# Moving the GEMM operands 32 bytes off the weights' place in SBUF, in a two-layer encoder trunk

## Chip, core and metric

The kernel runs on one core of one Trainium2 chip. The metric is the device time of one execution in microseconds (us), from launch to the last result. "Before" is the median of three timed runs; the trace is one further execution, recorded by the hardware profiler. Engines are named as in the profile: PE is the matrix engine, PEld its weight loads, DVE the vector engine, ACT the scalar engine, POOL the general-purpose one, SP the queue that issues the DMAs.

## The reference, cut to what matters

```python
D_MODEL, SEQ, DEPTH, D_FF = 2048, 256, 2, 8192
for i in range(DEPTH):
    u = rmsnorm(h, mix_norm_g[i])
    za, zh, zc, zr = split_last(u @ w_in[i], GROUP_SPLITS)      # 2048 x 6528
    ...                                                         # four mixers
    h = h + mix @ w_out[i]                                      # 2048 x 2048
    u = rmsnorm(h, mlp_norm_g[i])
    h = h + jnp.square(jax.nn.relu(u @ w_up[i])) @ w_down[i]    # 2048 x 8192, 8192 x 2048
    gate = jax.nn.sigmoid(rmsnorm(h, ple_norm_g[i]) @ w_ple_gate[i])   # 2048 x 2048
    h = h + (p[i] @ w_ple[i]) * gate
```

Everything is float32. There are 256 tokens, so each GEMM is a large weight matrix against a narrow activation.

## The kernel before

Activations lie transposed: channels on the 128 partitions, the 256 tokens (`S`) along the free axis, 16 chunks (`KC`) of 128 channels. Each GEMM keeps float32 accuracy with rounded operands (`F32R`): weight and activation are each split into a rounded part and the remainder. A weight unit of 1024 columns is loaded into `raw` (L135), ACT rounds each half of it into `wh` (L140) and DVE subtracts to get `wl` (L142). An activation chunk is a row of 512 columns, rounded part first and remainder behind it (`split`, L177).

One k-step multiplies one 128x128 weight block. There are two forms:

- `mm2` (L158, L159): `wh` against all 512 columns of the chunk, then `wl` against its first 256. Two weight loads and 768 columns.
- `mm3` (L150 to L152): three multiplications of 256 columns each (`wh` twice, `wl` once).

The weights are the stationary operand. The chunk of `u1`, `mh`, `u`, `act`, `ug` or `ph` is the moving operand, streamed past them. The next block's weights are loaded while a chunk streams.

The program runs stage after stage, twice, once for each layer:

- w_in and the mixers: moving operand `u1`, 15 output blocks by `mm3`, 36 by `mm2`, 16 k-steps each, between small float32 matmuls of the mixers.
- w_out: `mh1` by `mm2` (16 blocks of 12 k-steps), then `mh2` by `mm3` (16 blocks of 4).
- the MLP in four quarters: `up` (`u` into `act`) and `down` (`act` into `h`), each 16 blocks of 16 k-steps a quarter, all by `mm2`.
- the gate (`ug`, 16 blocks of 16 k-steps by `mm2`), mixed with w_ple (`ph`, 32 k-steps by `mm3`).

The moving operand `u` of a profile row is therefore one of two tiles (the profile drops numbers from names): `u1` in w_in, `u` in the MLP. Likewise `mh` is `mh1` at L158 and L159 and `mh2` at L150 to L152.

Tiles stand in pools, and a pool's place is set by the sizes of what was opened before it: `cp` (constants), `mp` (`h`, `u`, `ug`), `wp` (narrow weight buffers), then the pools of a stage (the wide weight buffers, `act`). The pool `up` with `u1` and `mh2`, and `op` with `mh1`, are allocated from the other end of SBUF. The order on each engine is the scheduler's; the functions below have the line numbers that the profile uses.

Of the kernel before, what the change touches and what calls it, by code (L numbers as in the profile page):

```python
# [8 lines left out]
F32 = mybir.dt.float32  # L9
# [7 lines left out]
P = 128  # L17
# [54 lines left out]
def trunk(ctx: ExitStack, tc: tile.TileContext, xT, pT, w_in, w_out1, w_out2, w_up, w_down, w_gate, w_ple, pvec,  # L72
          rel, lam, consts, lmask, onehot, lora, lorag, cw, outT, stages=None):
    nc = tc.nc
    V, A, G, T = nc.vector, nc.scalar, nc.gpsimd, nc.tensor

    cp = ctx.enter_context(tc.tile_pool(name="cp", bufs=1))
    mp = ctx.enter_context(tc.tile_pool(name="mp", bufs=1))
    wp = ctx.enter_context(tc.tile_pool(name="wp", bufs=3))
    sp = ctx.enter_context(tc.tile_pool(name="sp", bufs=4))  # L80
    pg = ctx.enter_context(tc.tile_pool(name="pg", bufs=2, space=PSUM))


    A.preload_act_table_set("natural_log_exp_and_others")
# [13 lines left out]
    def pc(l, n, i=0):  # L98
        o = l * NPC + POFF[n] + i
        return pv[:, o:o + 1]  # L100
# [60 lines left out]
    def add_to(dst, ps):  # L161
        V.tensor_tensor(dst, dst, ps[:, S:], ALU.add)
        V.tensor_tensor(dst, dst, ps[:, :S], ALU.add)  # L163

    def gemm_block(wsrc, m, act, mm=mm2, nk=KC, before=None):

        ps = K.accum("acc")
        for u in range(nk // 8):
            w = wsplit(wsrc[m, u])
            for j in range(8):  # L170
                k = u * 8 + j
                if before is not None:
                    before(k)
                mm(ps, w, j, act[:, k], k == 0, k == nk - 1)
        return ps

    def split(dst, src, scale=None):  # L177

        if scale is None:
            A.activation(dst[:, :S], src, AF.Copy)  # L180
            V.tensor_tensor(dst[:, S:], src, dst[:, :S].bitcast(F32), ALU.subtract)
        else:
            A.activation(dst[:, :S], src, AF.Identity, scale=scale)  # L183
            V.scalar_tensor_tensor(dst[:, S:], src, scale, dst[:, :S].bitcast(F32), ALU.mult, ALU.subtract)  # L184
# [36 lines left out]
    K = Ctx()  # L221
# [18 lines left out]
    def front():  # L240

        K.up_ = tc.tile_pool(name="up", bufs=1, side="right", reuse_waits="tile")
        K.up = K.up_.__enter__()
        K.u1 = K.up.tile([P, KC, 2 * S], F32R, tag="u1", name="u1")

    front()
    acc = sp.tile([P, S], F32, tag="ssacc", name="ssacc", bufs=1)

# [11 lines left out]
    for l in range(DEPTH):  # L260
# [53 lines left out]
        def norm():  # L314

            acc = sp.tile([P, S], F32, tag="ssacc", name="ssacc", bufs=1)
            for m in range(KC):
                sumsq(acc, h[:, m], m == 0)
            return rms_finish(acc, K.accum("ssq"))

        with tc.tile_pool(name="ap", bufs=2, reuse_waits="tile") as apool:
            NQ = 4
            acts, ahead, r = {}, [], None

            def up(q):
                nonlocal r
                acts[q] = apool.tile([P, 16, 2 * S], F32R, tag="act", name="act")
                if q == 0:
                    ahead.extend(gemm_block(w_up[l], f, u) for f in range(AHEAD))
                    r = norm()  # L330
                for f in range(16):
                    ps = ahead.pop(0) if ahead else gemm_block(w_up[l], q * 16 + f, u)
                    y = sp.tile([P, S], F32, tag="tmp", name="y", bufs=3)
                    A.activation(y, ps[:, S:], AF.Copy)
                    V.tensor_tensor(y, y, ps[:, :S], ALU.add)
                    V.scalar_tensor_tensor(y, y, 0.0, r, ALU.max, ALU.mult)
                    A.activation(y, y, AF.Square)
                    split(acts[q][:, f], y)

            def down(q):  # L340
                a = acts.pop(q)
                for m in range(KC):
                    ps = gemm_block(w_down[l, q], m, a)
                    add_to(h[:, m], ps)
                    if q == NQ - 1:
                        split(ug[:, m], h[:, m], pc(l, "pleg", m))
            up(0)
            for q in range(NQ):
                if q + 1 < NQ:
                    up(q + 1)  # L350
                else:
                    ug = mp.tile([P, KC, 2 * S], F32R, tag="u", name="ug")
                down(q)
# [12 lines left out]
        if l + 1 < DEPTH:  # L366
            front()
            acc = sp.tile([P, S], F32, tag="ssacc", name="ssacc", bufs=1)
# [75 lines left out]
class MixerD:  # L444
# [33 lines left out]
    def shift(self, m, blk, tag, bufs=1, ps=None):  # L478
        K, z, t = self.K, self.t1("z", 1), self.t1(tag, bufs)
        V, l, mu = K.nc.vector, K.l, K.pc  # L480
        if ps is None:
            K.z(m, z)
        else:
            V.tensor_tensor(z, ps[:, :S], K.r, ALU.mult)
        K.nc.scalar.activation(t, z, AF.Identity, scale=K.dcol(l, blk))
        V.scalar_tensor_tensor(t[:, 1:], z[:, :S - 1], mu(l, "mu0", blk), t[:, 1:], ALU.mult, ALU.add)
        V.scalar_tensor_tensor(t[:, :S - 1], z[:, 1:], mu(l, "mu1", blk), t[:, :S - 1], ALU.mult, ALU.add)
        return t
# [705 lines left out]
```

## Time and profile before

| | us |
|---|---|
| median of 3 runs | 2781.25 (2778.91 to 2785.14) |
| the profiled execution, its own time | 2778.84 |
| its span, first to last instruction | 2777.1 |
| PE busy | 2736.6 |
| DVE busy | 1986.5 |
| ACT busy | 1633.8 |

The recorded length of a matmul includes the drain of its results and overlaps the next one. The pace of PE is therefore read from the starts of neighbouring matmuls, not from their lengths; busy times of groups that alternate overlap and can't be added.

### The profile page before, as it was taken

How to read it: one execution, taken by the hardware profiler on the slowest of the kernel's cores; microseconds unless marked ns; L12 is line 12 of the kernel's file. 1: busy time of each engine (PE TensorE's matmuls, PEld its weight loads, DVE VectorE, ACT ScalarE, POOL GpSimd, SP SyncE). 2: the span in 40 equal slices, each digit the busy share in tenths (PEclk: the TensorE clock that was granted, in tenths of full speed). 3: DMA queues.
4: the chain of work that ended last, by engine and by line, in shares of the span. 5: the costliest groups of instructions: out<-in, count | busy, mean ns of one | idle time of the engine just before them, and what ended most of it. 6: DMA issues, size and time to landing. Idle time of an engine off the chain costs nothing.

```text
span 2777.1 us, 47281 instructions
## 1 busy us (share of the span) xinstructions
PE 2736.6 (99%) x16934; PEld 2361.7 (85%) x16934; DVE 1986.5 (72%) x4147; ACT 1633.8 (59%) x3342; POOL 54.5 (2%) x98
## 2 busy tenths in 40 slices
PE   8999999999999999999999999999999999999999
PEld 7878888888888888888898778888888888888887
DVE  8779777776666666677877797777766666666776
ACT  6656566566645546456765765565665465564565
POOL 0000110000000000000000011100000000000000
PEclk9999999999999999999999999999999999999999
DMA  6544454665555555555555454456655555555555
GB/s 221 169 132 159 152 166 151 218 199 184 189 183 189 185 187 187 185 189 192 175 168 162 140 165 142 164 163 191 195 185 188 185 189 184 189 186 186 186 198 160
DMA packets 187363, 495.45 MB, mean 178 GB/s; under 512 B 43860, under 2 KB 67028, under 8 KB 187000
## 3 DMA queue, kind: packets, MB, share of 16 engines
q1 hardware_dynamic: 187128, 492.44, 54.6%
q8 instruction: 133, 2.18, 0.3%
q14 instruction: 102, 0.84, 0.1%
HBM read 472.56 MB, written 19.80 MB: 177 GB/s over the span
## 4 chain that ended last, share of the span: by engine, by line
PE 89%; DVE 5%; ACT 2%; DMA 2%; issue 1%; SPq 0%; DVEq 0%; ACTq 0%
PE acc L158 49%; PE acc L159 25%; PE acc L152 2%; PE acc L150 2%; PE acc L151 2%; DVE wl L142 2%; PE psam L592 1%; PE psbl L1026 1%; ACT wh L140 1%; PE pss L757 1%; PE psrv L604 0%; DMA ot<-o_scr 0%; PE psy L780 0%; PE psl L936 0%; PE psrv L608 0%
## 5 line engine op out<-in xcount | busy, mean ns | idle before, releaser
L140 ACT ACTIVATE wh<-raw 128x512 fp32r<-128x512 f32 x1704 | 1076.5, 633 | 978.9 <-PE acc L158 831.1
L142 DVE TENSOR_TENSOR wl<-raw,wh 128x512 fp32r<-128x512 f32 x1704 | 1177.1, 692 | 631.4 <-ACT wh L140 620.4
L158 PE MATMUL acc<-u,wh 128*128 128x512 f32 x3200 | 1152.1, 401 | 4.9 <-ACT wh L140 4.0
L159 PE MATMUL acc<-u,wl 128*128 128x256 f32 x3200 | 917.9, 287 | 5.9 <-DVE wl L142 4.9
L158 PEld LDWEIGHTS acc<-u,wh 128*128 128x128 f32 x3200 | 601.2, 188 | 144.6 <-ACT wh L140 7.0
L158 PE MATMUL acc<-act,wh 128*128 128x512 f32 x2048 | 723.9, 399 | 0.0
L159 PEld LDWEIGHTS acc<-u,wl 128*128 128x128 f32 x3200 | 604.0, 189 | 23.9 <-DVE wl L142 16.4
L159 PE MATMUL acc<-act,wl 128*128 128x256 f32 x2048 | 575.2, 281 | 0.0
L158 PEld LDWEIGHTS acc<-act,wh 128*128 128x128 f32 x2048 | 384.8, 188 | 96.1
L159 PEld LDWEIGHTS acc<-act,wl 128*128 128x128 f32 x2048 | 386.9, 189 | 0.0
L158 PE MATMUL acc<-ug,wh 128*128 128x512 f32 x512 | 181.7, 398 | 0.0
L150 PE MATMUL acc<-u,wh 128*128 128x256 f32 x480 | 138.0, 287 | 10.7 <-ACT u L183 8.3
L152 PE MATMUL acc<-u,wl 128*128 128x256 f32 x480 | 140.8, 294 | 3.5 <-DVE wl L142 3.2
L159 PE MATMUL acc<-ug,wl 128*128 128x256 f32 x512 | 143.5, 281 | 0.0
L151 PE MATMUL acc<-u,wh 128*128 128x256 f32 x480 | 137.0, 285 | 0.8 <-DVE u L184 0.6
L158 PE MATMUL acc<-mh,wh 128*128 128x512 f32 x384 | 137.0, 396 | 0.7 <-DVE h L163 0.7
L158 PEld LDWEIGHTS acc<-ug,wh 128*128 128x128 f32 x512 | 96.0, 188 | 21.1
L159 PE MATMUL acc<-mh,wl 128*128 128x256 f32 x384 | 109.9, 287 | 1.4 <-DVE wl L142 1.2
L150 PEld LDWEIGHTS acc<-u,wh 128*128 128x128 f32 x480 | 91.3, 190 | 13.3 <-ACT u L183 8.3
L152 PEld LDWEIGHTS acc<-u,wl 128*128 128x128 f32 x480 | 91.0, 190 | 11.5 <-DVE wl L142 8.9
L159 PEld LDWEIGHTS acc<-ug,wl 128*128 128x128 f32 x512 | 96.7, 189 | 0.7
L151 PEld LDWEIGHTS acc<-u,wh 128*128 128x128 f32 x480 | 91.2, 190 | 2.0 <-DVE u L184 1.7
(321 smaller groups left out, 2738.4 us busy)
## 6 DMA issues: line engine op xcount, KB each, us to landing
raw<-in_w_up SPq DMA_DIRECT2D x256, 512.0 KB
raw<-in_w_down SPq DMA_DIRECT2D x256, 512.0 KB
raw<-in_w_in SPq DMA_DIRECT2D x204, 512.0 KB
raw<-in_w_gate SPq DMA_DIRECT2D x64, 512.0 KB
raw<-in_w_out SPq DMA_DIRECT2D x32, 512.0 KB
raw<-in_w_out SPq DMA_DIRECT2D x64, 256.0 KB
h<-in_xT SPq DMA_DIRECT2D x8, 512.0 KB
m_scr<-sp SPq DMA_DIRECT2D x16, 256.0 KB
```

Of the source, the lines that this page charges most:

```text
L140: A.activation(wh[:, :n], raw[:, o:o + n], AF.Copy)
L142: V.tensor_tensor(wl[:, :n], raw[:, o:o + n], wh[:, :n].bitcast(F32), ALU.subtract)
L150: T.matmul(ps[:, :S], w1, act[:, :S], start=start, stop=False)
L151: T.matmul(ps[:, :S], w1, act[:, S:], start=False, stop=False)
L152: T.matmul(ps[:, :S], w2, act[:, :S], start=False, stop=stop)
L158: T.matmul(ps, wh[:, b * P:(b + 1) * P], act, start=start, stop=False)
L159: T.matmul(ps[:, :S], wl[:, b * P:(b + 1) * P], act[:, :S], start=False, stop=stop)
L592: T.matmul(pm[h][:, x * S:(x + 1) * S], BK[HS[h], j, x, :], KR[j][HS[h]].rearrange("p a b -> p (a b)"), start=True, stop=True)
L757: T.matmul(ps[:, d * P + h * 64:d * P + (h + 1) * 64], Zs[d][:, h * 2 + j, :], rk(d, j)[:, h] if st == 0 else RH[:, d, h, :], start=True, ...
L1026: T.matmul(p2[:, i * P:(i + 1) * P], kc[:, i * P:(i + 1) * P], strided(Q, i * P, [[2 * hh, P // (2 * hh)], [W + hh, 2], [1, hh]]), start=T ...
```

## The change

It adds empty tiles ahead of four pools' contents. `shift` allocates one tile of the given number of float32 columns and sets it to zero once, so that the scheduler sees it used.

```diff
+    def shift(pool, cols):
+
+        V.memset(pool.tile([P, cols], F32, tag="pad", name="pad", bufs=1), 0.0)
+
+    shift(cp, 24)
+    shift(wp, 24)
...
         K.u1 = K.up.tile([P, KC, 2 * S], F32R, tag="u1", name="u1")
+        shift(K.up, 16)
...
         with tc.tile_pool(name="ap", bufs=2, reuse_waits="tile") as apool:
+            shift(apool, 8)
```

`shift(K.up, ...)` and `shift(apool, ...)` run once in each layer, so six memsets are added in all. No matmul, DMA or conversion is added, removed or changed in order; what changes is the byte address of nearly every tile in its partition. For the operands of the GEMMs the built programs place:

```
tile (where it moves or is weight)   before        mod 128   after         mod 128
wh, wl narrow (w_in, first of w_out)  96448...          64    96640...           0
wh, wl wide (w_out on, MLP, gate)    127168...          64   127360...           0
u1, mh2 (w_in, w_out by mm3)         196576             96   196512             32
mh1 (w_out by mm2)                   172000             96   171936             32
u, ug (up, gate)                      47296             64    47392             32
act, two buffers (down)              143552, 176320     64   143776, 176544     32
ph (w_ple)                           145600             64   145792              0
```

A chunk is 2048 bytes and a weight block 512, so all chunks of a tile and all blocks of a buffer have the same place modulo 128. The moving operand's place less the weights' is 32 bytes before for `u1`, `mh1` and `mh2`, and 0 for `u`, `ug`, `act` and `ph`. After the change it is 32 for all but `ph`, where it stays 0.

The order differs on DVE alone. This is the last part of w_out in layer 0, where `act`'s pool opens, before (`h`, `u`, `ssacc` and `sq` belong to the residual and its sum of squares):

```order
L184 SCALAR_TENSOR_TENSOR u<-h,pv,u 128x256
L308 TENSOR_TENSOR h<-h,acc 128x256
L142 TENSOR_TENSOR wl<-raw,wh 128x512
L184 SCALAR_TENSOR_TENSOR u<-h,pv,u 128x256
L142 TENSOR_TENSOR wl<-raw,wh 128x512
```

And the same place after the change, where all lines of the file stand 7 or 8 further down:

```order
L191 SCALAR_TENSOR_TENSOR u<-h,pv,u 128x256
L316 TENSOR_TENSOR h<-h,acc 128x256
L85 MEMSET pad 128x8
L149 TENSOR_TENSOR wl<-raw,wh 128x512
L191 SCALAR_TENSOR_TENSOR u<-h,pv,u 128x256
L149 TENSOR_TENSOR wl<-raw,wh 128x512
```

One memset has come in between two instructions whose order is as it was; its other places, two at the start, one behind the first constants and one in the gate of layer 0, look the same.

## Rows read from the trace of the kernel before

**Rows 1.** The page: span, PE's busy time, the chain that ended last by engine.

```profile
span 2777.1 us, 47281 instructions
PE 2736.6 (99%) x16934; PEld 2361.7 (85%) x16934; DVE 1986.5 (72%) x4147; ACT 1633.8 (59%) x3342; POOL 54.5 (2%) x98
...
PE 89%; DVE 5%; ACT 2%; DMA 2%; issue 1%; SPq 0%; DVEq 0%; ACTq 0%
```

**Rows 2.** Busy time by stretch: w_out (two), up, down twice, gate.

```profile
core 0: us, PE busy (x) PEld busy (x) DVE busy (x) ACT busy (x) POOL busy (x), PEclk, DMA share, GB/s
521.90:546.50 24.60, 24.60 (x143) 21.81 (x142) 16.76 (x31) 10.78 (x17) 0.00 (x0) 1.00 0.59 171
546.70:568.90 22.20, 22.20 (x192) 22.20 (x192) 21.76 (x51) 17.80 (x38) 0.00 (x0) 1.00 0.68 202
...
841.60:931.80 90.20, 90.20 (x512) 78.28 (x511) 60.21 (x111) 55.58 (x109) 0.00 (x0) 1.00 0.56 186
1113.00:1293.60 180.60, 180.60 (x1024) 156.58 (x1023) 124.37 (x222) 92.81 (x161) 0.00 (x0) 1.00 0.57 186
1293.80:1392.00 98.20, 98.20 (x589) 87.04 (x588) 79.58 (x166) 73.60 (x160) 0.53 (x1) 1.00 0.54 178
```

**Rows 3.** PE's groups by line and shape: busy us, mean ns, idle before.

```profile
L158 PE MATMUL acc<-u,wh 128*128 128x512 f32 x3200 | 1152.1, 401 | 4.9 <-ACT wh L140 4.0 <-DVE x L232 0.9
...
L158 PE MATMUL acc<-act,wh 128*128 128x512 f32 x2048 | 723.9, 399 | 0.0
L159 PE MATMUL acc<-act,wl 128*128 128x256 f32 x2048 | 575.2, 281 | 0.0
L158 PE MATMUL acc<-ug,wh 128*128 128x512 f32 x512 | 181.7, 398 | 0.0
...
L158 PE MATMUL acc<-mh,wh 128*128 128x512 f32 x384 | 137.0, 396 | 0.7 <-DVE h L163 0.7
```

**Rows 4.** Timeline of PE (start us, length us): an unbroken run of w_out.

```profile
521.90 0.28 PE L159 MATMUL acc<-mh,wl 128*128 128x256 f32 x1
...
546.52 0.28 PE L159 MATMUL acc<-mh,wl 128*128 128x256 f32 x1
```

**Rows 5.** Timeline of PE: first and last k-step of two quarters of down.

```profile
1112.88 0.40 PE L158 MATMUL acc<-act,wh 128*128 128x512 f32 x1
...
1293.44 0.40 PE L158 MATMUL acc<-act,wh 128*128 128x512 f32 x1
```

**Rows 6.** Timeline of PE: the second quarter of up, first and last k-step.

```profile
841.52 0.40 PE L158 MATMUL acc<-u,wh 128*128 128x512 f32 x1
...
931.62 0.40 PE L158 MATMUL acc<-u,wh 128*128 128x512 f32 x1
```

**Rows 7.** Timeline of PE: w_out by mm3, first and last matmul.

```profile
546.64 0.28 PE L150 MATMUL acc<-mh,wh 128*128 128x256 f32 x1
...
568.92 0.28 PE L152 MATMUL acc<-mh,wl 128*128 128x256 f32 x1
```

**Rows 8.** Timeline of PE in the gate: one group of w_ple by mm3.

```profile
1305.44 0.28 PE L150 MATMUL acc<-ph,wh 128*128 128x256 f32 x1
...
1306.87 0.40 PE L158 MATMUL acc<-ug,wh 128*128 128x512 f32 x1
```

**Rows 9.** Timeline of PE in w_in, between two small matmuls of the mixers.

```profile
449.93 0.39 PE L158 MATMUL acc<-u,wh 128*128 128x512 f32 x1
450.16 0.28 PE L159 MATMUL acc<-u,wl 128*128 128x256 f32 x1
450.28 0.40 PE L158 MATMUL acc<-u,wh 128*128 128x512 f32 x1
450.51 0.28 PE L159 MATMUL acc<-u,wl 128*128 128x256 f32 x1
450.63 0.40 PE L158 MATMUL acc<-u,wh 128*128 128x512 f32 x1
```

**Rows 10.** Timeline of PE: plain float32 matmuls of the mixers, merged.

```profile
1626.16 1.03 PE L1045 MATMUL psbo<-bAT,x 128*128 128x256 f32 x4
...
1713.20 0.59 PE L793 MATMUL psm<-t,cst 128*128 128x256 f32 x2
```

**Rows 11.** DVE's groups by line and shape: one subtraction on three tiles.

```profile
L181 DVE TENSOR_TENSOR act<-y,act 128x256 fp32r<-128x256 f32 x128 | 53.7, 419 | 0.2
...
L181 DVE TENSOR_TENSOR mh<-ot,mh 128x256 fp32r<-128x256 f32 x32 | 13.2, 425 | 10.4 <-ACT mh L180 10.4
```

**Rows 12.** Timeline of DVE: the first memsets.

```profile
0.90 0.17 DVE L93 MEMSET onesd<- 128x128 f32 x1 [0.90 <-PEq L1181]
...
1.07 0.06 DVE L550 MEMSET cum<- 128x2 f32 x1
```

## The prediction

> **What bounds the kernel now.** I read the page first: PE is busy for 2736.6 of 2777.1 us and holds 89% of the chain that ended last [rows 1]. So the time is, but for some 5% of DVE and 2% each of ACT and DMA, a sum of matmul steps. The table by stretch says where nothing else can be late: in up, down and gate PE is busy for the whole of each stretch, DVE for 67 to 81% of it and ACT for 51 to 75%, the DMA engines move 178 to 187 GB/s, and the granted clock is 1.00, that is 2.4 GHz, throughout [rows 2]. The groups agree: 0.0 us of idle ahead of the matmuls of `act` and `ug` [rows 3]. What remains is how long PE takes for one k-step when nothing makes it wait, and this must be read from starts.
>
> An `mm2` k-step in `down`: from 1112.88 to 1293.44 us lie 511 steps (two quarters of 16 blocks of 16 are 512 steps, and these are the starts of the first and the last), 180.56 / 511 = 353.35 ns [rows 5]. In `up`: 90.10 us over 255 steps, 353.33 ns [rows 6]. The same `mm2` step in w_out: 143 matmuls [rows 2] start from 521.90 to 546.52 us [rows 4], so 71 steps in 24.62 us, 346.8 ns. Same lines, same shapes, same wide weight buffers, same clock, and 6.55 ns apart. The lengths in the groups don't show this (399 and 396 ns at L158 [rows 3]); only the starts do.
>
> What differs is in the table of places. `mh1` stands 32 bytes behind the weights modulo 128, `u` and `act` stand at the same place. The `mm3` form says the same once more: 191 gaps of `mh2`, 32 behind, take 22.28 us, 116.6 ns each [rows 7]; 12 gaps of `ph`, difference 0, take 1.43 us, 119.2 ns each [rows 8]. So the trace of before holds the experiment already: two tiles at 32 and three at 0, all 0s slow, all 32s fast. The place in SBUF at large doesn't sort them: `u` lies at 47 kB, one `act` buffer at 143 kB and the other at 176 kB, inside the range of `mh1` (172 to 197 kB), and `u` and `act` have the same step. Nor does the neighbours' load: the fastest `mm3` stretch is the one in which DVE is busy for 21.76 of 22.20 us and the DMA engines move 202 GB/s [rows 2].
>
> **The change, part by part.** *Moved to a difference of 32: `u`, `act`, `ug`.* Up has 4 x 16 x 16 = 1024 k-steps in a layer, down as many, the gate 256; two layers make 2048 + 2048 + 512 = 4608 (the counts at L158 are 2048 for `act` and 512 for `ug` [rows 3]). All are on the path. At 353.35 - 346.8 = 6.55 ns each: 4096 x 6.55 = 26.8 us in the MLP, 512 x 6.55 = 3.4 us in the gate, 30.2 us in all. The price of a step at difference 32 in these stages isn't in the trace, since none runs there so; the nearest row is the 346.8 of w_out, with the same weight buffers and no interruption. The far bound is w_in, where the mixers' small matmuls come in between: two steps of 0.35 us from 449.93 to 450.63 [rows 9], 350 ns, also at difference 32. I take 346.8 because the MLP has no interruption. By 350 the gain would be 4608 x 3.35 = 15.4 us. On the other side a step can't be expected to fall below what the same form takes at the same difference, so 346.8 is also the near end.
>
> What is next behind PE when it speeds up by 1.9%: the conversions and the weights. DVE would be busy for 79.58 of some 96.5 us in the gate, 82%, and for 69% in up; the transfers would rise from 187 to 190 GB/s, and 202 are seen [rows 2]. None becomes late; were the gate held at its present pace by DVE all the same, its 3.4 us would be missing.
>
> *Left alone: `u1`, `mh1`, `mh2` (32 before and after) and `ph` (0 before and after).* Their 1536 `mm2` and 672 `mm3` k-steps keep their difference, so I count 0, on the condition that it is the difference that matters and not the place itself (a rival below).
>
> *The mixers' plain float32 matmuls.* Their operands' differences change too, mostly among multiples of 32. Two neighbours show what that is worth: four at difference 0 take 1.03 us and two at 64 take 0.59 us [rows 10]; the two more cost 0.44, 0.22 us each, and taking one step of 0.22 from either leaves the same tail of 0.37. I count 0 here, with half a microsecond either way.
>
> *DVE, ACT, DMA.* The same subtraction takes 419 ns on `act` (all operands at 64) and 425 ns on `mh` (32 apart) [rows 11], 1.4%. On the 5% of the chain that DVE holds, 139 us [rows 1], that is at most 2 us either way; I count 0, since most of those instructions don't change their operands' differences. Landing places of the DMAs change as well and no row compares them; on the 2% of the chain that is DMA, 56 us, the same 1.4% would be 0.8 us either way.
>
> *Six memsets.* The rows bracket one between 0.06 and 0.17 us [rows 12], so 0.4 to 1.0 us of DVE in all. Two stand at the start ahead of the constants while PE waits for its first data, the one in w_out stands where DVE is nearly full (98% [rows 2]), so up to 0.2 us of it may be on the path. They wait for nothing new, and PE gets no new wait. I count 0.
>
> The sum against the profiled execution: 2778.84 - 30.2 = 2748.6 us. The median of before is 2.4 us above that execution: 2781.25 - 30.2 = 2751.0 us.
>
> **The rivals.** *No change.* The 6.55 ns belong to the stage and not to the address: the MLP is the only long stretch without a pause, and PE might settle there into a slower pattern whatever the addresses are. For it: no MLP stretch at 32 exists, and the 71 fast steps [rows 4] are a short run beside 511 [rows 5]. Against it: `ph` is slow in groups of 12 [rows 8] while 192 matmuls of `mh2` in a row stay fast [rows 7]. Then it stays at 2781. The Trainium skill speaks for this one. Its page "SBUF — State Buffer", section "SBUF: two separate sides", says of PE that it never waits on anyone for its ports, and "TensorE: Matmul & The Clock Gate", section "Step-by-step: what each phase is for", says that the moving operand and the weight load have a read port each, so that loading the next weights takes nothing from the running matmul. By that rule the addresses would be worth nothing and the time 2781 us; the steps above, 353.35 against 346.8 ns, don't agree with it as far as this trace goes.
>
> *Slower.* Not the difference but the absolute place makes a step fast: a moving operand at 96 against weights at 64. After the change no operand is there (all at 32, weights at 0). Then up, down and gate stay as they are and w_in and w_out fall to the slow step: 1536 x 6.55 = 10.1 us for `mm2` and 608 x 3 x (119.2 - 116.6) = 4.7 us for `mm3`, 14.8 us in all, 2796 us. It decides from the point where w_out's step is above some 350 ns. For it: all fast steps of before have the one pair (96, 64). Against it: the pair (32, 0) is the same pair moved by 64, and nothing in the rows singles out the upper half of 128 bytes.
>
> *Half the gain.* The step at 32 in the MLP comes out at the 350 ns of w_in, because the blocks' ends or the w_ple groups disturb it: 2781.25 - 15.4 = 2766 us. It is the far end of the forecast's own range.
>
> **How the numbers follow.** The forecast with its bounds, a gain of 15 to 37 us, gets 0.80; no change 0.10; slower 0.05; a gain outside these bounds 0.05. The predicted time is the forecast's, 2751. The range: upwards to the step of 350, 2766; downwards the small terms (2 + 0.8 + 0.5 us) and the spread of the runs of before (their lowest is 2.3 us below the median) on top of the gain, 2751 - 5.6, and a little more for rounding, 2744. It leaves out 0.2. A measurement of this kernel can tell about 0.2%, 5.6 us, from no change. Faster by more: 0.80 + 0.05 = 0.85; within: 0.10; slower: 0.05.
>
> **What would show it.** In the trace of the changed kernel two quarters of down in a row should take 511 x 0.3468 = 177.2 us from first to last start, not 180.6; the MLP of one layer some 13.4 us less; w_out's step still 346.8, its `mm3` gaps 116.6 and `ph`'s 119.2. Down at 353 with w_out at 347 is the first rival; w_out at 353 is the second; down at 350 the third. The prediction is wrong in its root if `ph`, whose difference doesn't change, gets faster too: then the place itself counts, and not the difference.

## The result and the profile after

The changed kernel takes 2751.07 us (median of 4 runs, 2749.29 to 2752.99), the kernel before 2781.59 in the same series (4 runs, 2778.91 to 2785.14). The ratio is 0.989, with a 95% interval of 0.9873 to 0.9907. That is 30.5 us between the medians; 2751.0 us was forecast. The profiled execution took 2751.58 us, its span is 2749.9.

The page of the changed kernel: the span, the busy times (us, share, instructions), the chain that ended last by engine, and the two groups of PE that answer to [rows 3] (busy us, mean ns of one, idle ahead of them):

```profile
span 2749.9 us, 47287 instructions
...
PE 2709.4 (99%) x16934; PEld 2363.0 (86%) x16934; DVE 1983.7 (72%) x4153; ACT 1631.2 (59%) x3342; POOL 54.6 (2%) x98
...
PE 90%; DVE 4%; DMA 2%; ACT 2%; issue 1%; SPq 0%; DVEq 0%; ACTq 0%
...
L165 PE MATMUL acc<-act,wh 128*128 128x512 f32 x2048 | 710.2, 390 | 0.0
...
L165 PE MATMUL acc<-ug,wh 128*128 128x512 f32 x512 | 179.4, 393 | 0.0
```

PE is busy for 27.2 us less than in [rows 1], and the span is 27.2 us shorter. The kernel is still a sum of matmul steps, and the matmuls of `act` and `ug` still wait for nothing. The timeline of PE says where the time went. First, as in [rows 5], [rows 6] and [rows 7], the first and last matmul (start us, length) of `up`, of two quarters of `down`, and of w_out by `mm3`:

```profile
836.59 0.40 PE L165 MATMUL acc<-u,wh 128*128 128x512 f32 x1
...
925.00 0.39 PE L165 MATMUL acc<-u,wh 128*128 128x512 f32 x1
...
1102.86 0.39 PE L165 MATMUL acc<-act,wh 128*128 128x512 f32 x1
...
1280.01 0.39 PE L165 MATMUL acc<-act,wh 128*128 128x512 f32 x1
```

```profile
547.47 0.28 PE L157 MATMUL acc<-mh,wh 128*128 128x256 f32 x1
...
569.76 0.28 PE L159 MATMUL acc<-mh,wl 128*128 128x256 f32 x1
```

Up: 88.41 us over 255 steps, 346.7 ns (353.3 before). Down: 177.15 over 511, 346.7 (353.35 before). `mh2`, whose difference did not change: 22.29 over 191, 116.7, as before. From the start of one stage to the start of the next, the parts of the span moved so (us, from the same starts in both traces):

```
                                     before            after            change
MLP, layer 0 and layer 1         724.76  723.93    710.48  710.48       -27.7
gate with w_ple, both layers     102.02  102.19    100.97  100.85        -2.4
start, w_in with mixers, w_out  1117.6 in all     1120.5 in all         +2.9
```

The rest, 6.6 us behind the gate's last step, is the same in both. The third row is no effect of the change that I can show: in a later execution of the same changed kernel it comes to 1117.6, and the difference lies mostly in w_in and the mixers.

What stands behind PE, by stretch (us; busy us and count for PE, PEld, DVE, ACT, POOL; granted clock; DMA share; GB/s), for up, down and the gate:

```profile
836.60:925.20 88.60, 88.60 (x513) 77.99 (x512) 59.94 (x112) 55.56 (x109) 0.00 (x0) 1.00 0.59 190
1102.90:1280.20 177.30, 177.30 (x1025) 157.19 (x1024) 124.31 (x223) 92.61 (x161) 0.00 (x0) 1.00 0.59 190
1280.40:1378.00 97.60, 97.60 (x591) 87.13 (x591) 79.86 (x168) 73.48 (x160) 0.55 (x2) 1.00 0.55 179
```

PE has no gap, the granted clock is 1.00 (2.4 GHz) as in [rows 2], DVE is at 82% in the gate, and the transfers deliver 190 GB/s in up. Nothing became late.

### The profile page after: what moved, and what is told of

It is laid out like the page before. It is cut to its first block, busy times and chain, and to the rows that moved or that the text cites. A ratio compares the mean times of both kernels' runs of the same rounds, so it can differ in the third digit from the quotient of the medians.

```text
span 2749.9 us, 47287 instructions
## 1 busy us (share of the span) xinstructions
PE 2709.4 (99%) x16934; PEld 2363.0 (86%) x16934; DVE 1983.7 (72%) x4153; ACT 1631.2 (59%) x3342; POOL 54.6 (2%) x98
## 4 chain that ended last, share of the span: by engine, by line
PE 90%; DVE 4%; DMA 2%; ACT 2%; issue 1%; SPq 0%; DVEq 0%; ACTq 0%
PE acc L165 48%; PE acc L166 26%; PE acc L159 3%; PE acc L157 2%; PE acc L158 2%; DVE wl L149 1%; PE psam L601 1%; PE psbl L1035 1%; PE pss L766 1%; DMA ot<-o_scr 1%; ACT wh L147 1%; PE psrv L613 0%; DMA raw<-in_w_out 0%; PE psy L789 0%; PE psl L945 0%
## 5 line engine op out<-in xcount | busy, mean ns | idle before, releaser
L165 PE MATMUL acc<-u,wh 128*128 128x512 f32 x3200 | 1140.1, 397 | 5.4 <-ACT wh L147 4.5
L165 PE MATMUL acc<-act,wh 128*128 128x512 f32 x2048 | 710.2, 390 | 0.0
```

Source lines behind the costliest of these rows:

```text
L165: T.matmul(ps, wh[:, b * P:(b + 1) * P], act, start=start, stop=False)
```

## Experiments

**A bare stream.** The same `mm2` step, 64 times in each of 31 series that differ in their places, with no conversion, no DMA and no pause beside it; ACT copies one result at the end of each series:

```python
for k in range(64):
    T.matmul(ps, wt[:, h + j * 128:...], mv[:, m:m + 512], ...)         # j = k % 16
    T.matmul(ps[:, :S], wt[:, l + 4096 + j * 128:...], mv[:, m:m + 256], ...)
```

> This kernel leaves out the whole model. It holds two tiles of weights and one of activations in SBUF and runs 31 series of 64 mm2 k-steps each (512 columns against one block, 256 against another) with no DMA, no conversion and no wait beside them; each series has its own place of the moving operand and its own difference to the weights, and the output holds a part of each series' sums. Theory (it is the difference modulo 128 bytes, and PE alone): the series at difference 0, 128, 256 and 1024 take 353 ns a step, the one at 32 takes 347, at every place of the moving operand (0, 32, 64, 96); what 4 to 28 and 36 to 124 take is open, and 64 and 96 should be at 347 or below if 32 bytes are the unit. Rival 1 (the absolute place): difference 32 gives 347 only with the moving operand at 32 or 96, and series of the same difference differ by place. Rival 2 (it needs the neighbours' reads and writes or the stream of new weights): all series take the same, near 347. The two last series set the difference for wh and wl apart; if the loss arises while wl loads under the 512 columns, the series with wl at 0 and wh at 32 takes 353 and the other 347.

Measured, from the starts, ns a step:

```
difference     0     4     8    12    16    20    24    28    32    36    40
           353.4 353.3 351.7 346.7 353.3 353.3 349.6 348.8 346.7 348.9 350.0
difference    48    56    64    72    80    96   112   124   128   256  1024
           353.2 352.0 353.3 350.0 346.7 353.2 346.6 350.1 351.1 353.4 353.4
moving at 32, 64, 96, difference 0: 353.4 each;  difference 32: 346.6, 346.7, 346.7
wh 0, wl 32: 346.6;  wh 32, wl 0: 346.7
```

Two of these series in the stream's timeline, first and last start: difference 0 with both at place 32, and difference 32 with the moving operand at 0:

```profile
533.57 0.39 PE L107 MATMUL serax<-mv,wt 128*128 128x512 f32 x1
...
555.83 0.40 PE L107 MATMUL serax<-mv,wt 128*128 128x512 f32 x1
```

```profile
219.40 0.40 PE L107 MATMUL seraj<-mv,wt 128*128 128x512 f32 x1
...
241.26 0.39 PE L107 MATMUL seraj<-mv,wt 128*128 128x512 f32 x1
```

22.26 us over 63 steps is 353.3 ns, 21.86 is 347.0 (346.7 without its first steps). The effect needs no neighbours and no long stage, and moving both operands together leaves it: the rivals of the stage and of the absolute place fall. But 32 is no threshold either: 12, 80 and 112 are as fast as 32, and 16, 48 and 96 as slow as 0. And here one operand apart is enough: the reason I had thought of (a loss while `wl` loads under the 512 columns) asked for a slow step at (`wh` 32, `wl` 0), and it is fast.

**All at one place.** In the kernel itself, every difference 0 modulo 128, with the places still moved by the pads of `cp` and `up`:

```diff
     shift(cp, 24)
-    shift(wp, 24)
...
-            shift(apool, 8)
```

> The changed kernel without the pads of wp and ap: all GEMM operands and all weights stand at 32 modulo 128, so every difference is 0, u1, mh1 and mh2 included. Theory (difference): up, down and gate take 353.3 ns a step as before the change, and w_in and w_out lose too: 1536 mm2 steps x 6.55 ns = 10.1 us and 608 mm3 steps x 3 x 2.6 ns = 4.7 us, at most 14.8 us above the kernel before, 2790 to 2796 us, less where w_in waits for other engines anyway. Rival (absolute place, moving operand at 32 is fast): as the changed kernel, 2751 us.

Measured 2785.82 us (12 runs), ratio 1.0022 (1.0012 to 1.0032): 4.8 us above the kernel before, not at the 2790 to 2796 that I expected. Up and down are at 353.3 to 353.4 as before the change. What is slower is w_out and, between the mixers, w_in (uninterrupted steps 350.4 ns on average, 348.4 before). Here is the `mm3` of `mh2`, first and last start:

```profile
553.29 0.27 PE L156 MATMUL acc<-mh,wh 128*128 128x256 f32 x1
...
575.95 0.28 PE L158 MATMUL acc<-mh,wl 128*128 128x256 f32 x1
```

22.66 us over 191 gaps, 118.6 ns against 116.7; the unbroken `mm2` steps of w_out take 351.1 (24.93 us over 71), not 353.4. The `mh` and `u1` of this kernel differ from the weights by 0 modulo 128 but by 128 modulo 256, and the stream gives 351.1 at a difference of 128. That was the first sign that 128 is not the whole period.

**The pad of `act` left out.** `act` goes back to a difference of 0, all else stays as changed:

```diff
         with tc.tile_pool(name="ap", bufs=2, reuse_waits="tile") as apool:
-            shift(apool, 8)
```

> The changed kernel without the 32 bytes ahead of act alone: act stands at 0 as its weights do, all else as changed. Theory: the 2048 k-steps of down go back to 353.3 ns, up and gate stay at 346.9: 2751.1 + 2048 x 6.5 ns = 2764.4 us. Rival (PE settles into a pattern that runs on over stages): up slows too or down stays fast, 2751 or 2781 us.

Measured 2764.0 us (6 runs), ratio 0.9944 (0.9928 to 0.9959). One execution now holds both paces. Its timeline, up and then down:

```profile
837.55 0.40 PE L165 MATMUL acc<-u,wh 128*128 128x512 f32 x1
...
925.97 0.39 PE L165 MATMUL acc<-u,wh 128*128 128x512 f32 x1
...
1105.53 0.40 PE L165 MATMUL acc<-act,wh 128*128 128x512 f32 x1
...
1286.07 0.40 PE L165 MATMUL acc<-act,wh 128*128 128x512 f32 x1
```

Up 88.42 / 255 = 346.7 ns, down 180.54 / 511 = 353.3. One tile's place sets its own stage's pace and no other's, and `down` is worth 12.9 us (2764.0 less 2751.1), about half of the gain.

**Other differences in the kernel.** `u`, `u1`, `mh` and `ug` at 64 modulo 128, `act` at 96:

```diff
-    shift(wp, 24)
+    shift(wp, 16)
...
-            shift(apool, 8)
+            shift(apool, 24)
```

> The changed kernel with other pads: u, ug, u1, mh1 and mh2 stand 64 bytes behind the weights modulo 128 and act 96. Theory with 32 bytes as the unit: both are as good as 32, each stage 346.9 ns, 2751 us. If only 32 is good: up and gate or down at 353.3, 2765 to 2790 us. If a larger difference is better still, a step below 346 ns and a time below 2749 us.

Measured 2777.49 us (12 runs), ratio 0.9991 (0.998 to 1.0001). Up runs at 353.3, down at 350.0, `mh2`'s `mm3` at 117.8. Down gains half of what 32 gives it, up nothing, and w_in and w_out lose. "Apart" is not the rule; of the three values other than 0 that were timed in the kernel here, only 32 brings the gain.

**Both weights apart.** The bare stream with the differences of `wh` and `wl` varied on their own, 0 to 112 in steps of 16, 48 steps a series:

> This kernel leaves out the whole model and holds the bare stream of mm2 steps of the first sweep, 64 series of 48 steps: the differences of the moving operand to wh and to wl go through 0, 16, ... 112 bytes independently. The first sweep gave three levels, 346.7, 350.0 and 353.3 ns. Theory (two reads collide as long as all three operands keep the same lanes): only (0, 0) and its like, where both differences are equal, reach 353.3, and most pairs of unequal differences take 346.7. Rival (one pair decides, wl against the 512 columns that stream while it loads): one whole row or column of the map is slow. If any pair is below 346 ns, 32 bytes isn't the best place.

The 64 steps lie between 343.4 (`wh` 32, `wl` 96) and 354.8 ns, mostly at 346.7, 350 or 353.3, with no order that I can read. Equal differences are not singled out: (16, 0) is 353.3, (48, 32) is 353.3, (112, 112) is 346.7. My rule fell.

**Other forms and types**, each alone in a stream, differences 0, 16, ..., 112:

> This kernel leaves out the whole model and runs bare streams of one form of matmul, 64 matmuls a series, at differences 0, 16, ... 112: mm3 as in w_ple, then 512, 256 and 128 columns of rounded float32, the same of bfloat16, and 256 columns of plain float32. Theory (the reads of moving operand and of the next weights meet): rounded float32 loses some 2 ns a matmul of 256 at difference 0 (119.2 against 116.6 in mm3) and a like share at 512; plain float32, which streams at half the rate, loses nothing (215 to 216 at any difference); bfloat16 is open. Rival (the loss needs the alternation of 512 and 256 columns): 512 alone takes the same at all differences.

```
ns a matmul              0     16     32     48     64     80     96    112
F32R, mm3            120.0  120.0  118.7  118.8  117.8  118.3  118.4  118.3
F32R, 256 columns    120.0  120.0  118.7  118.8  117.8  118.3  118.4  118.4
F32R, 512 columns    226.9  233.3  234.2  232.0  233.3  233.3  233.3  233.3
F32R, 128 columns    111.7  at every difference
bf16, 512 / 256 / 128 columns    215.8 / 109.2 / 55.8  at every difference
plain float32, 256 columns       215.8 a recorded pass, two passes a matmul, at every difference
```

In the bf16 series of 512 columns the trace has 62 or 63 of the 64 matmuls; where one is missing the two starts beside it are 431 ns apart, twice 215.8, and these gaps are left out. The groups of the two 512-column rounded series at 0 (first) and 32, where the busy time of 64 matmuls is 63 steps and one length:

```profile
L115 PE MATMUL seraj<-mv,wt 128*128 128x512 f32 x64 | 14.7, 390 | 0.0
...
L115 PE MATMUL seral<-mv,wt 128*128 128x512 f32 x64 | 15.2, 396 | 0.0
```

(14.7 - 0.39) / 63 = 227 ns, (15.2 - 0.40) / 63 = 235. Of these types only rounded float32 feels the place, from 256 columns on, and with 512 columns alone the sign is the other way round: level is the fast case. So nothing as simple as "level operands collide" can be the reason.

**`wl` alone apart, then `wh` alone apart**, in the kernel. The first puts a pad between the wide `wh` and `wl`, so that in the MLP and the gate `wh` is level modulo 128 and `wl` 32 off; the second has it the other way round, with a pad of 8 columns there, one of 24 ahead of the wide buffers, and none ahead of `act`. This is the first one's edit:

```diff
-    shift(wp, 24)
...
+            if K.w_bufs == W_WIDE and K.padded is not K.rawp:
+                K.padded = K.rawp
+                shift(K.rawp, 24)
             wl = K.rawp.tile([P, 512], F32R, tag="wl", name="wl", bufs=K.w_bufs)
```

> The kernel with all at zero difference, but wl of the wide weight buffers moved by 96 bytes, so that up, down and gate have wh at difference 0 and wl at 32. By the bare stream (346.6 ns for this pair) one of the two apart is enough: MLP and gate at 346.9, some 30 us below the 2785.8 of all at zero, 2756 us. Rival (each load must be apart from its own stream, wh against the 256 columns included): MLP stays at 353 or comes to 350, 2771 to 2786 us.

> The mirror: in up, down and gate wh stands at difference 32 and wl at 0, all else at zero difference. By the bare stream (346.7 ns) again 2756 us. Rival (wl loads while the 512 columns stream, and there the loss arises): 353 in the MLP, 2786 us.

Measured 2762.21 us (4 runs), ratio 0.9936 (0.992 to 0.9953), and 2762.13 (4 runs), 0.9941 (0.992 to 0.9961). With `wl` apart, down runs at 346.7. Up does so only in its first two quarters, which run back to back ahead of the first of down; the third and the fourth, with the same tiles at the same places, do not. The first two from the norm's matmul on (480 steps) and the third (256 steps) in the timeline; [rows 6], headed as the second quarter, is the third as well:

```profile
582.29 0.58 PE L167 MATMUL acc<-u,wh 128*128 128x512 f32 x1
...
748.53 0.39 PE L167 MATMUL acc<-u,wh 128*128 128x512 f32 x1
...
837.63 0.39 PE L167 MATMUL acc<-u,wh 128*128 128x512 f32 x1
...
927.29 0.40 PE L167 MATMUL acc<-u,wh 128*128 128x512 f32 x1
```

166.24 / 479 = 347.1 ns and 89.66 / 255 = 351.6. So one pair of places can have more than one steady pace. With `wh` apart, up runs at 350.7 to 351.1 and down at 344.5, below any step seen in the kernel so far, though `u` and `act` have equal differences modulo 128. They differ modulo 256: `act`'s differences to (`wh`, `wl`) are (32, 0), `u`'s (160, 128).

**The map over 512 bytes.** The bare stream again, both differences from 0 to 480 in steps of 32, 40 steps for each of 256 pairs:

> This kernel leaves out the whole model: the bare stream of mm2 steps again, 256 series of 40 steps, with the differences of the moving operand to wh and to wl taken modulo 512 in steps of 32 bytes. In the kernel with wh apart, act (moving operand less wh 32, less wl 0, modulo 256) took 344.6 ns and u (160 and 128) 350.9, though both pairs are (32, 0) modulo 128. Theory (the period is longer than 128 bytes): the series (32, 0) takes some 344.6 and (160, 128) some 351, and the map repeats with 256. Rival (the difference modulo 128 decides, and the two levels come from the stage's start): both series take the same, and the map repeats with 128. If a pair takes 344 or less at all its repeats, it is a candidate for a kernel better than both: 4608 steps x 2.7 ns = 12 us.

It repeats with 256 bytes, in both directions, but for two entries: (0, 0) at 353.3 and (0, 256) at 346.7, (32, 0) at 344.4 and (32, 256) at 346.7. One period, ns a step, `wh`'s difference down, `wl`'s across:

```
         0     32     64     96    128    160    192    224
  0  353.3  353.3  351.1  346.7  346.7  346.7  346.7  346.7
 32  344.4  346.7  353.3  346.7  348.9  346.7  346.7  348.9
 64  340.0  348.9  353.3  349.5  346.7  348.9  346.7  346.7
 96  349.2  346.7  353.3  350.0  346.7  353.3  348.9  346.7
128  352.0  346.6  346.7  351.1  351.1  351.7  346.7  352.0
160  346.7  346.7  348.3  353.3  351.1  346.7  348.0  343.3
192  340.0  351.1  353.3  346.7  353.3  353.3  353.3  346.7
224  351.1  346.7  351.1  350.7  353.3  350.0  348.3  353.3
```

Two of its series in the timeline, (64, 0) and (64, 64):

```profile
477.72 0.39 PE L105 MATMUL serbh<-mv,wt 128*128 128x512 f32 x1
...
490.98 0.39 PE L105 MATMUL serbh<-mv,wt 128*128 128x512 f32 x1
...
505.28 0.39 PE L105 MATMUL serbj<-mv,wt 128*128 128x512 f32 x1
...
519.05 0.39 PE L105 MATMUL serbj<-mv,wt 128*128 128x512 f32 x1
```

13.26 / 39 = 340.0 ns and 13.77 / 39 = 353.1 (353.3 without its first steps). By its places, the first stream's 32 is (160, 160) here, its 64 (192, 192) and its 96 (224, 224), and they agree. The map gives the pace of most stages seen so far: before, `u` and `act` (0, 0) 353.3; after, `u` (160, 160) and `act` (32, 32) 346.7; without `act`'s pad `act` (0, 0) again; at 64 and 96 `u` (192, 192) 353.3 and `act` (96, 96) 350.0; with `wh` apart `act` (32, 0) 344.4 (measured 344.5) and `u` (160, 128) 351.1 (350.7). With `wl` apart `act` (128, 32) is 346.6 as measured, and `u` (0, 160) 346.7 in the first two quarters alone.

But the map is not the whole answer, and the two other streams say so. At the same addresses, byte for byte, (0, 160) took 346.7 in the first stream and in the map and 351.8 in the second; (192, 224) took 346.7 in the map and 351.1 in the second stream; (192, 0) took 340.0 in the map and 350.0 in the second stream. First and last start of (192, 0), second stream (48 steps), then map (40):

```profile
572.00 0.40 PE L105 MATMUL serbh<-mv,wt 128*128 128x512 f32 x1
...
588.45 0.39 PE L105 MATMUL serbh<-mv,wt 128*128 128x512 f32 x1
```

```profile
3156.80 0.39 PE L105 MATMUL serir<-mv,wt 128*128 128x512 f32 x1
...
3170.05 0.39 PE L105 MATMUL serir<-mv,wt 128*128 128x512 f32 x1
```

16.45 / 47 = 350.0 ns and 13.25 / 39 = 339.7 (340.0 by the unrounded starts). Nothing but ACT's copy of the series before runs beside either; they differ in what PE ran ahead of them. So several paces for one pair need no busy neighbours.

**The map's best pair in the kernel**, every moving operand 64 bytes behind `wh` and level with `wl`:

```diff
-    shift(cp, 24)
-    shift(wp, 24)
+    shift(wp, 48)
...
+            if all(p is not K.rawp for p in K.padded):
+                K.padded.append(K.rawp)
+                V.memset(K.rawp.tile([P, 16], F32, tag="mid", name="pad", bufs=1), 0.0)
             wl = K.rawp.tile([P, 512], F32R, tag="wl", name="wl", bufs=K.w_bufs)
...
-        shift(K.up, 16)
+        shift(K.up, 8)
...
                 K.raw_bufs, K.w_bufs = RAW_WIDE, W_WIDE
+                shift(K.rawp, 48)
...
-            shift(apool, 8)
```

> The whole kernel with every moving operand, ph included, 64 bytes behind wh and at the same place as wl, modulo 256. In the bare stream this pair took 340.0 ns in all of its repeats, against 346.7 for the changed kernel's places. Theory (the step is set by the two differences modulo 256 and nothing else): up, down and gate take 340.0 to 340.3 ns a step, 4608 x 6.7 = 30.7 us below the changed kernel, 2720 us; w_in and w_out, 1536 mm2 steps, give up to 10 us more, 2710 to 2720. Rival (346.7 is a floor in the kernel, where conversions write the weights while they are read): 2745 to 2751 us. Rival (the conversions or the weights' DMAs become late): steps above 340 with idle time ahead of L158's or L159's successors, waiting for ACT, DVE or raw.

Measured 2760.77 us (5 runs), ratio 0.9932 (0.9918 to 0.9946), 40 to 50 us short of what I expected. The timeline of PE where the MLP begins, around the residual norm's small matmul:

```profile
579.62 0.39 PE L167 MATMUL acc<-u,wh 128*128 128x512 f32 x1
...
579.96 0.39 PE L167 MATMUL acc<-u,wh 128*128 128x512 f32 x1
...
580.30 0.39 PE L167 MATMUL acc<-u,wh 128*128 128x512 f32 x1
580.52 0.28 PE L168 MATMUL acc<-u,wl 128*128 128x256 f32 x1
580.64 0.59 PE L218 MATMUL ssq<-ssacc,onesd 128*128 128x256 f32 x2
580.88 0.58 PE L167 MATMUL acc<-u,wh 128*128 128x512 f32 x1
581.30 0.28 PE L168 MATMUL acc<-u,wl 128*128 128x256 f32 x1
581.42 0.40 PE L167 MATMUL acc<-u,wh 128*128 128x512 f32 x1
...
581.77 0.40 PE L167 MATMUL acc<-u,wh 128*128 128x512 f32 x1
```

Steps of 340 ns before `ssq`, 350 after it, and 350.0 from there to the end of the MLP in every quarter of both layers, with no wait. The gate's uninterrupted steps take 343.3 on average. The 72 unbroken steps of w_out, at one and the same pair of places, take 340.1 in layer 0 and 350.0 in layer 1 (and in the next experiment 350.0 and 340.0).

**The norm's matmul elsewhere.** As the last, and `ssq` put between the two matmuls of a later step, so that the `wl` part follows it:

```diff
-                    ahead.extend(gemm_block(w_up[l], f, u) for f in range(AHEAD))
-                    r = norm()
+                    def mm2n(ps, parts, b, act, start, stop):
...
+                        T.matmul(ps, wh[:, c * P:(c + 1) * P], act, start=start, stop=False)
+                        if len(seen) == 3:
+                            r = norm()
+                        T.matmul(ps[:, :S], wl[:, c * P:(c + 1) * P], act[:, :S], start=False, stop=stop)
+                    ahead.extend(gemm_block(w_up[l], f, u, mm2n if f == AHEAD else mm2) for f in range(AHEAD + 1))
```

> The kernel before this one (every moving operand 64 bytes behind wh and level with wl, modulo 256) with one thing more: the norm's small matmul at the start of each layer's MLP stands between the wh and the wl matmul of one k-step of the third block of up, where it stood between two k-steps. In the trace of the run before, PE runs at 340 ns a step up to that matmul and at 350 from it on to the end of the MLP; in the gate the norm's matmul falls between wh and wl, and the steps behind it take 340. Theory (the addresses allow more than one steady pattern, and what interrupts PE last decides which): up and down take 340.0 to 340.3 ns, 4096 x 10 = 41 us below 2760.8, so 2720 us, 29 us below the changed kernel. Rival (the pattern comes from the stage's addresses or its neighbours): 350 ns and 2761 us again.

Measured 2756.17 us (6 runs), ratio 0.9922 (0.9904 to 0.994). My expectation of 2720 fell:

```profile
581.13 0.39 PE L348 MATMUL acc<-u,wh 128*128 128x512 f32 x1
...
581.47 0.39 PE L348 MATMUL acc<-u,wh 128*128 128x512 f32 x1
...
581.81 0.40 PE L348 MATMUL acc<-u,wh 128*128 128x512 f32 x1
582.05 0.60 PE L218 MATMUL ssq<-ssacc,onesd 128*128 128x256 f32 x2
582.29 0.47 PE L351 MATMUL acc<-u,wl 128*128 128x256 f32 x1
582.60 0.40 PE L348 MATMUL acc<-u,wh 128*128 128x512 f32 x1
...
582.95 0.40 PE L348 MATMUL acc<-u,wh 128*128 128x512 f32 x1
```

Again 340 before and 350 after. The same block of the same stage, with the same tiles, changes its pace at one interruption and keeps the new one for the rest of the MLP. Which pace follows an interruption, and why, stays open.

The trace of the kernel before holds the same thing, at difference 0. Its gate, around the norm's matmul:

```profile
1293.79 0.40 PE L158 MATMUL acc<-ug,wh 128*128 128x512 f32 x1
...
1299.44 0.40 PE L158 MATMUL acc<-ug,wh 128*128 128x512 f32 x1
1299.68 0.59 PE L209 MATMUL ssq<-ssacc,onesd 128*128 128x256 f32 x2
...
1300.93 0.39 PE L158 MATMUL acc<-ug,wh 128*128 128x512 f32 x1
...
1305.10 0.39 PE L158 MATMUL acc<-ug,wh 128*128 128x512 f32 x1
```

5.65 / 16 = 353.1 ns ahead of `ssq`, 4.17 / 12 = 347.5 behind it, with level operands in both, and 353.3 again behind the next group of w_ple. In up it is the other way round: six steps ahead of `ssq`, from 578.61 to 580.69 us, take 346.7, and all behind it 353.3. So level operands have two paces, and in the MLP of before `ssq` leaves PE in the slower one. For the pairs of the changed kernel, (32, 32) and (160, 160), all streams and traces show 346.7 as the only steady pace. Of 53 timed executions of the kernel before with a granted clock of 0.998 or more, four took 2765 to 2772 us, about what one layer's MLP at 346.7 would give; no trace of such a one was kept, so this is not shown.

**The changed kernel once more**, on the chip of the best pair's runs:

> The changed kernel unaltered, on the same chip as the run beside it: 2751 us and 346.9 ns a step by every theory.

2749.15 us (4 runs), ratio 0.9887 (0.9874 to 0.9901), up and down at 346.7 again. It is the best version: none of the experiments beats it.

## Why the prediction was right, and where it was not

*What bounds the kernel.* Right: PE's busy time and the span fell by the same 27.2 us, and nothing else moved by more than the mixers' own spread.

*The MLP's term, 26.8 us.* Right: 27.7 measured, 13.4 to 14.3 a layer. 0.8 of it is no pace: in layer 0 of before, PE waited once for `wh` (0.55 us idle ahead of 572.76 us), which no other trace shows there. The pace alone gives 26.9. The step came out at 346.7, the 346.8 of w_out [rows 4], and not at the 350 of w_in [rows 9]. That choice was the one that mattered. The two steps of [rows 9] stand beside small matmuls of the mixers; the uninterrupted steps of w_in take 348.4 on average at the pair of w_out.

*The gate's term, 3.4 us.* A little too large: 2.4 measured. I multiplied its 512 steps by the MLP's 6.55 ns, but the gate is broken up by w_ple's groups, and some of its stretches ran near 347 before the change already; its uninterrupted steps took 352.4 ns on average before and 348.0 after, 4.4 apart. 512 x 4.4 = 2.3 us. Its cover held: DVE at 82%, as worked out, and no wait.

*The small terms.* The unbroken steps of `mh1` (346.7 before, 346.7 to 347.0 after) and the gaps of `mh2` kept their times; memsets, DVE and DMA show nothing beyond the spread of w_in and the mixers.

*The rivals.* "No change" fell in the kernel: the MLP is as long and as even as before and runs at 346.7, and the bare stream shows both paces without a neighbour. With it the Trainium skill's rule, "SBUF — State Buffer", section "SBUF: two separate sides", that PE never waits for anyone, does not cover what the runs show: 353.4 and 346.7 ns in streams beside which ACT alone works, for one copy a series. But a part of that rival was right: the 353.3 of the MLP before did not belong to the address alone, since the same places also ran at 346.7. "Slower", by the absolute place, fell in the stream at places 32, 64 and 96 (353.4 each at difference 0) and in the kernel with everything at 32 modulo 128, where `u` and `act` stay at 353.3.

*Where the explanation was too narrow.* I read two tiles at 32 and three at 0 as a rule: 32 bytes apart modulo 128 is fast, level is slow. The numbers followed from these two values only, and both held for this change. The rule does not. The pace hangs on the differences of `wh` and of `wl` modulo 256, without visible order, and on what PE ran before; of the types tried only rounded float32 shows it; and level is the fast case for 512 columns alone. "All 0s slow" was not even true of the trace of before, whose gate and up have level steps at 346.7. More than half of the gain rested on luck: modulo 256 the changed kernel has `act` at 32, the pair of `mh1` that the 346.8 was read from, but `u` and `ug` at 160, a pair that no row of before had timed. That 160 takes 346.7, too, could not be known; (128, 128), as level as (0, 0) by my rule, takes 351.1. With pads for 64 and 96 bytes, the same reasoning, read as "apart is fast", would have promised 30 us, and 2777.49 came out.

*The test that I set myself.* I wrote that the prediction would be wrong in its root if `ph` got faster. It did, a little: its uninterrupted gaps went from 119.1 to 118.3 ns, though its difference is 0 before and after. It is not the absolute place modulo 128: with all at 32 modulo 128 `ph` stands elsewhere too and takes 119.1. What goes along with it, in all six traces that have `ph` level, is the pace of the gate's `mm2` steps around it (352 with 119.0 to 119.1, 348 with 118.3). That it takes over something of its neighbours' pattern fits, and is not shown.

*What stays open.* Why these places give these paces; and what chooses among several paces for the same places after an interruption. The streams show that it takes no busy neighbour.

## What to carry to other kernels

Read a matmul's pace from starts, stage by stage; where two stages of the same form in rounded float32 differ by some 2% with nothing waiting, compare where their moving and stationary tiles begin, modulo 256, before you look for a busy neighbour. A bare stream over the differences maps this in one run, but it only names candidates: the pair at 340 ns in the stream gave 350 in the kernel, and the change's own pairs at 346.7 held in both of its traces, so every candidate has to be timed in place. Run each pair more than once, behind different work: a pair with two paces in the streams can settle in the slower one. In bf16 and plain float32 the runs show no such effect at differences of 0 to 112, so they give no reason to move anything.

## What the runs showed of the hardware

- A rounded-float32 step of 768 columns takes 340 to 355 ns in streams with no conversion and no DMA beside them, by the operands' places and by what PE ran before, at a granted clock of 1.00. At 2.4 GHz the common paces are whole numbers of cycles: 340.0, 343.3, 346.7, 350.0 and 353.3 ns are 816, 824, 832, 840 and 848, eight apart.
- The same places can run at 340 or at 350 ns, before and after a single small matmul, and the step did not come back to 340 in the 2000 steps to the end of the MLP. Level operands do the same at 346.7 and 353.3.
- With a weight load ahead of every matmul, bf16 takes 215.8, 109.2 and 55.8 ns for 512, 256 and 128 columns, rounded float32 227 to 234, 118 to 120 and 111.7: at 128 columns twice as long, and independent of place.
